# Small TensorE products held into bursts, and one transpose pass per gated block, in a two-layer hybrid encoder

## Chip, cores and metric

The kernel runs on one core of a Trainium2 chip. The metric is the device time of one execution in microseconds (us), as the median of several runs.

## What is computed

256 tokens of width 1024 pass through two layers. Each layer has a gated FFN half-step, a mixer of three branches, and a second FFN half-step; everything is float32.

```python
for i in range(DEPTH):
    h = rms_norm(x, ffn1_norm[i])
    x = x + 0.5 * (silu(h @ w_gate) * (h @ w_up)) @ w_down     # D_FF = 2816
    h = rms_norm(x, mix_norm[i])
    s5_u, gla_q, ..., at_v = split(h @ w_in[i])
    y_s5, y_gla, y_attn = s5_branch(s5_u), gla_branch(...), attn_branch(...)
    gates = sigmoid(h @ w_merge_gate[i] + b_merge_gate[i])
    x = x + sum(gate_b * (y_b @ w_branch_b)) @ w_out[i]
    x = x + 0.5 * ffn2(rms_norm(x, ffn2_norm[i]))
return rms_norm(x, final_norm)
```

The S5 branch is a bidirectional complex-diagonal state space with 32 groups of 16 channels and 64 states. Its tables (input and output matrices, powers of the decay) depend only on parameters.

## The kernel before

**Large products.** Every weight is split into two fp32r parts, `hi` (a cast on ScalarE, L209) and `lo` (a subtraction on VectorE, L210), and so is the activation. A product is three matmuls of 128x128 by 128x512 (`mm3`, L219 to L221): hi by hi, hi by lo, lo by hi. `stream` (from L223) goes through blocks of 512 output columns, loading two k-rows of weights per DMA on SP's queue (L206; five raw buffers, four cast ones), and calls the block's evacuation for each of the two token halves (t = 0, 1). In PSUM, accumulators come from a pool of three banks (`pmm`), small products from one of three (`psm`), transposes from one of two (`ptr`).

**FFN.** A block holds 256 gate and 256 up columns. Its evacuation (`evac`, L290) runs per token half: SiLU on ScalarE (L294), product on VectorE (L295), two 128x128 transposes on TensorE (L298), a cast on ScalarE (L300) and a subtraction on VectorE (L301) that write `sTh` and `sTl`, which the down product reads as activation. There are 11 blocks per FFN and four FFNs.

**S5 tables.** `s5_tables` (L529) prepares each layer's tables in four quarters of eight groups, in steps woven between the FFN's large products: layer 0's into its first FFN, layer 1's into layer 0's second FFN and layer 1's first. For a quarter VectorE makes `bb` and, from it, `tb`, which is stored in the tile that later becomes `cc`. Eight transposes (L585) go through two `psm` banks, and ScalarE copies them to `ld["bb"]` (L586). Then VectorE makes `cc`, real part first, and TensorE forms `kp`: L597 (128x32 by 128x32) and L603 (64x32 by 64x96), each as two records in the trace. ScalarE and VectorE copy `kp` to `ks` (L607 to L610), and the tables are stored to DRAM on SP's queue.

**S5 branch.** `s5` runs four quarters per layer. TensorE makes `S` (L820), VectorE multiplies, scans and multiplies again, which gives `X0` (tile `t2`) and then `X1` (`t4`). Two banks `yp` take three products for each of two halves i: `U` with `mt` (L855, 64x64), `X0` and `X1` with `cc` (L858, 128x64). `U` and `mt` are there long before, `X1` is made last. ScalarE copies `yp` to `yg` (L861), and after the fourth quarter a GELU follows.

**What sets the order.** The kernel hands its instructions to a builder that orders each engine's queue by a simulated timeline (`schedule_with_timeline_sim=True`). An instruction written earlier goes first where several are ready; one that is ready while the earlier ones are not may go ahead of them. In the mixer the branches' steps are written with raised priority (`weave` with `high_priority`); in the FFNs the tables' steps are not.

## Time and profile before

| | |
|---|---|
| median of 3 runs | 1358.05 us (1356.56 to 1358.73) |
| profiled execution | 1357.79 us |
| its span, first to last instruction | 1356.0 us |
| mean granted TensorE clock | 0.995 |
| TensorE busy | 1310.3 us, 6792 records |
| VectorE busy | 1013.2 us |
| ScalarE busy | 703.5 us |
| DMA | 249.87 MB, mean 184 GB/s |

The busy time of TensorE (PE) counts overlapping matmuls as one stretch, and the ends of matmuls are modelled. So what a matmul costs is read from the distance between starts, not from its duration. In a timeline, instructions of one form that follow one another stand as one line with their count.

### The profile page before, as it was taken

What the parts mean: (1) busy time and instruction counts of PE and PEld (TensorE: products, weight loads), DVE (VectorE), ACT (ScalarE), POOL (GpSimd) and SP (SyncE); (2) the same over time, 40 slices, a digit from 0 to 9 for tenths busy, and PEclk for the clock granted to TensorE, in tenths of its full rate; (3) what the DMA queues carried; (4) which work ended last, traced back from release to release, by engine and by line L of the source; (5) the groups of instructions that cost most, each with busy time, mean ns of one, the idle gap of its engine ahead of it and who ended that gap; (6) DMA issues with size and microseconds to landing.
All of it is one profiled execution on the core that took longest, in us unless ns stands there. A gap on an engine that the chain in (4) does not pass through costs nothing.

```text
span 1356.0 us, 19228 instructions
## 1 busy us (share of the span) xinstructions
PE 1310.3 (97%) x6792; PEld 1049.8 (77%) x6792; DVE 1013.2 (75%) x1794; ACT 703.5 (52%) x1106; POOL 76.9 (6%) x108
## 2 busy tenths in 40 slices
PE   7999999999999989999999999999999999999997
PEld 5877778877786778777877777888877867888886
DVE  6899985779995779997465765457899967655553
ACT  5545445547585445444354544355475854555542
POOL 1010220000100000210000000000001000000000
PEclk9999999999999989999999999999999999999999
DMA  7767666666452366666665655566665524555562
GB/s 230 189 214 232 219 226 189 202 223 218 163 182 78 117 161 208 196 208 215 195 196 180 196 164 189 187 177 217 226 210 156 174 68 148 191 177 181 183 209 77
DMA packets 201200, 249.87 MB, mean 184 GB/s; under 512 B 40856, under 2 KB 134600, under 8 KB 201104
## 3 DMA queue, kind: packets, MB, share of 16 engines
q1 hardware_dynamic: 200496, 247.59, 58.6%
q8 instruction: 53, 0.87, 0.3%
q10 hardware_dynamic: 608, 1.06, 0.2%
q14 instruction: 43, 0.35, 0.1%
HBM read 234.44 MB, written 13.11 MB: 183 GB/s over the span
## 4 chain that ended last, share of the span: by engine, by line
PE 58%; issue 18%; DVE 17%; DMA 4%; ACT 3%; POOL 1%; SPq 0%; POOLq 0%; ACTq 0%; DVEq 0%
PE mm L220 17%; PE mm L219 16%; PE mm L221 16%; DVE lo L210 5%; DVE t L349 2%; DMA raw<-in_ffn_w_gate 1%; DVE run L838 1%; DMA e<-scr 1%; PE as L1072 1%; PE ao L1094 1%; DVE run L837 1%; PE st L298 1%; ACT hi L209 1%; DMA raw<-in_ffn_w_up 1%; PE pt L263 1%
## 5 line engine op out<-in xcount | busy, mean ns | idle before, releaser
L210 DVE TENSOR_TENSOR lo<-raw,hi 128x1024 fp32r<-128x1024 f32 x412 | 499.0, 1218 | 178.8 <-ACT hi L209 174.1
L209 ACT CAST hi<-raw 128x1024 fp32r<-128x1024 f32 x412 | 427.8, 1043 | 309.0 <-PE mm L221 282.4
L220 PE MATMUL mm<-lo,hTh 128*128 128x512 f32 (+1 forms) x1120 | 444.0, 397 | 7.6 <-DVE lo L210 7.4
L219 PE MATMUL mm<-hi,hTh 128*128 128x512 f32 (+1 forms) x1120 | 436.4, 396 | 2.0 <-ACT hTh L267 2.0
L221 PE MATMUL mm<-hi,hTl 128*128 128x512 f32 (+1 forms) x1120 | 435.1, 392 | 0.0
L220 PEld LDWEIGHTS mm<-lo,hTh 128*128 128x128 f32 x1120 | 211.4, 189 | 53.0 <-DVE lo L210 11.9
L219 PEld LDWEIGHTS mm<-hi,hTh 128*128 128x128 f32 x1120 | 211.1, 189 | 44.4 <-ACT hTh L267 2.9
L221 PEld LDWEIGHTS mm<-hi,hTl 128*128 128x128 f32 x1120 | 210.7, 188 | 40.1 <-DVE hTl L268 0.2
L220 PE MATMUL mm<-lo,sThffn 128*128 128x512 f32 x352 | 138.3, 393 | 2.8 <-DVE lo L210 2.8
L221 PE MATMUL mm<-hi,sTlffn 128*128 128x512 f32 x352 | 137.4, 391 | 0.0
L219 PE MATMUL mm<-hi,sThffn 128*128 128x512 f32 x352 | 135.9, 393 | 0.0
L300 ACT CAST sThffn<-st 128x256 fp32r<-128x256 f32 x88 | 32.7, 372 | 129.9 <-PE st L298 129.5
L220 PEld LDWEIGHTS mm<-lo,sThffn 128*128 128x128 f32 x352 | 66.1, 188 | 17.7 <-DVE lo L210 3.7
L221 PEld LDWEIGHTS mm<-hi,sTlffn 128*128 128x128 f32 x352 | 66.1, 188 | 13.9
L219 PEld LDWEIGHTS mm<-hi,sThffn 128*128 128x128 f32 x352 | 66.0, 188 | 13.6
L301 DVE TENSOR_TENSOR sTlffn<-st,sThffn 128x256 fp32r<-128x256 f32 x88 | 37.1, 423 | 48.8 <-ACT sThffn L300 48.3
L294 ACT ACTIVATE t<-mm,rstd 128x256 f32<-128x256 f32 x88 | 41.5, 475 | 43.5 <-PE mm L221 41.1
L295 DVE SCALAR_TENSOR_TENSOR t<-mm,rstd,t 128x256 f32<-128x256 f32 x88 | 41.8, 482 | 13.6 <-ACT t L294 13.4
L298 PE MATMUL st<-ident,t 128*128 128x128 f32 x176 | 33.4, 272 | 0.5 <-DVE t L295 0.5
L298 PEld LDWEIGHTS st<-ident,t 128*128 128x128 f32 x176 | 24.3, 140 | 12.1 <-DVE t L295 0.9
L349 DVE TENSOR_TENSOR t<-e,S 128x512 f32<-128x512 f32 x32 | 20.2, 683 | 17.3 <-DMA e<-scr 17.2
L627 POOL COPY kx<-ks 128x128 f32<-128x128 f32 x32 | 18.9, 630 | 218.7 <-DVE ks L610 218.7
(357 smaller groups left out, 1440.0 us busy)
## 6 DMA issues: line engine op xcount, KB each, us to landing
raw<-in_ffn_w_gate SPq DMA_DIRECT2D x176, 256.0 KB, 3.8
raw<-in_ffn_w_up SPq DMA_DIRECT2D x176, 256.0 KB, 4.3
raw<-in_ffn_w_down SPq DMA_DIRECT2D x88, 512.0 KB, 4.6
raw<-in_w_in SPq DMA_DIRECT2D x48, 512.0 KB, 3.9
raw<-in_w_merge_gate SPq DMA_DIRECT2D x48, 512.0 KB, 4.6
raw<-in_w_out SPq DMA_DIRECT2D x16, 512.0 KB, 4.4
scr<-e SPq DMA_DIRECT2D x6, 768.0 KB, 5.5
e<-scr SPq DMA_DIRECT2D x6, 768.0 KB, 5.7
```

The source lines that it names most:

```text
L209: nc.scalar.copy(hi[:, :e - s, :width], raw[:, :e - s, :width])
L210: nc.vector.tensor_tensor(lo[:, :e - s, :width], raw[:, :e - s, :width], hi[:, :e - s, :width].bitcast(F32), op=ALU.subtract)
L219: nc.tensor.matmul(ps, act[0], w[0], start=first, stop=False)
L220: nc.tensor.matmul(ps, act[0], w[1], start=False, stop=False)
L221: nc.tensor.matmul(ps, act[1], w[0], start=False, stop=last)
L294: nc.scalar.activation(sg, ps[:, :256], AF.Silu, scale=rstd[:, t:t + 1])
L295: nc.vector.scalar_tensor_tensor(s, ps[:, 256:], rstd[:, t:t + 1], sg, op0=ALU.mult, op1=ALU.mult)
L298: nc.tensor.transpose(pt[:, j], s[:, j * P:(j + 1) * P], self.ident)
L300: nc.scalar.copy(h, pt)
L301: nc.vector.tensor_tensor(sl[:, 2 * b:2 * b + 2, t * P:(t + 1) * P], pt, h.bitcast(F32), op=ALU.subtract)
L349: self.nc.vector.tensor_tensor(out, a, b, op=ALU.mult)
L627: nc.gpsimd.tensor_copy(kx[:, :, s], ks.rearrange("p g j f -> p g (j f)")[:, :, (3 - s) * 16:(3 - s) * 16 + 64])
```

## The change

In the FFN, `evac` keeps the gated product of t = 0 until that of t = 1 is there, and then issues four transposes into one bank, those of t = 1 first, each held behind the one before; one cast and one subtraction follow. In `s5_tables`, `tb` gets a tile of its own; `kp` starts with L603 (the imaginary part, made last, first), then L597, then the eight transposes, each of the latter two held behind what was issued before; the second transposed half uses a bank of `ptr`. In `s5`, the products of `X1` come first and start the accumulation, then `X0`, then `U`. "Held" (`behind`) is an edge for the builder's order alone; it adds no wait on the chip.

```diff
+    def behind(self, m, prev):
+        self.tc.add_manual_dep(m.ins, prev.ins.name,
+                               mybir.DependencyInfo(mybir.DependencyClass.NoSync, mybir.DependencyReason.DATA),
+                               reason="one burst")
+        return m
...
             def evac(b):
+                s = []
                 def f(t, ps):
-                    self.n += 1
-                    sg, s = self.t2([P, 256]), self.t2([P, 256])
+                    sg = self.t2([P, 256])
+                    s.append(self.t2([P, 256]))
...
-                    pt = self.ptr.tile([P, 2, P], F32, name=f"st{self.n}", tag="tr")
-                    for j in range(2):
-                        nc.tensor.transpose(pt[:, j], s[:, j * P:(j + 1) * P], self.ident)
-                    h = sh[:, 2 * b:2 * b + 2, t * P:(t + 1) * P]
-                    nc.scalar.copy(h, pt)
-                    nc.vector.tensor_tensor(sl[:, 2 * b:2 * b + 2, t * P:(t + 1) * P], pt, h.bitcast(F32),
-                                            op=ALU.subtract)
+                    if t < NT - 1:
+                        return
+                    pt = self.ptr.tile([P, 2, SEQ], F32, name=self.nm("st"), tag="tr")
+                    m = None
+                    for i in range(NT - 1, -1, -1):
+                        for j in range(2):
+                            x = nc.tensor.transpose(pt[:, j, i * P:(i + 1) * P], s[i][:, j * P:(j + 1) * P], self.ident)
+                            m = self.behind(x, m) if m else x
+                    self.split_into(sh[:, 2 * b:2 * b + 2], sl[:, 2 * b:2 * b + 2], pt)
...
-            tb = ld["cc"].rearrange("p (r a e t f) -> p r a e t f", r=2, a=4, e=2, t=4)
+            tb = pp.tile([P, 2, 4, 2, 4, 16], F32, name=self.nm("tb"), tag="tb")
...
-            for i in range(2):
-                ps = self.psm.tile([P, 4, P], F32, name=self.nm("bT"), tag="sm")
-                src = tb[:, i].rearrange("p a e t f -> p a (e t f)")
-                for a in range(4):
-                    nc.tensor.transpose(ps[:, a], src[:, a], self.ident)
-                nc.scalar.copy(ld["bb"].rearrange("p (a r m) -> p r a m", a=4, r=2)[:, i], ps)
...
-            for i in range(2):
-                for a in range(4):
-                    lt = bb[:, i, 2 * a:2 * a + 2].rearrange("p e f -> p (e f)")
-                    nc.tensor.matmul(kp[0][a * 32:(a + 1) * 32, :, 0], lt, cpar[:, 2 * i, :, a], start=i == 0, stop=i == 1)
-            for i in range(2):
+            for i in (1, 0):
                 for a in range(4):
                     for d in range(2):
...
-                        nc.tensor.matmul(kp[d][a * 32:(a + 1) * 32, :, 1 - d:4 - d], lt, c5[rows, i, :, a, d:d + 3],
-                                         start=i == 0, stop=i == 1)
+                        m = nc.tensor.matmul(kp[d][a * 32:(a + 1) * 32, :, 1 - d:4 - d], lt, c5[rows, i, :, a, d:d + 3],
+                                             start=i == 1, stop=i == 0)
+            for i in range(2):
+                for a in range(4):
+                    lt = bb[:, i, 2 * a:2 * a + 2].rearrange("p e f -> p (e f)")
+                    m = self.behind(nc.tensor.matmul(kp[0][a * 32:(a + 1) * 32, :, 0], lt, cpar[:, 2 * i, :, a],
+                                                     start=i == 0, stop=i == 1), m)
+            for i in range(2):
+                pool, tag = ((self.psm, "sm"), (self.ptr, "tr"))[i]
+                ps = pool.tile([P, 4, P], F32, name=self.nm("bT"), tag=tag)
+                src = tb[:, i].rearrange("p a e t f -> p a (e t f)")
+                for a in range(4):
+                    m = self.behind(nc.tensor.transpose(ps[:, a], src[:, a], self.ident), m)
+                nc.scalar.copy(ld["bb"].rearrange("p (a r m) -> p r a m", a=4, r=2)[:, i], ps)
...
+                for r, X in ((1, X1), (0, X0)):
+                    for g, h, a, o in gh:
+                        nc.tensor.matmul(o, X[:, g * 4 + a], cc[:, r, g * 4 + a], start=r == 1, stop=False)
                 for g, h, a, o in gh:
                     rows = slice(g * 64, g * 64 + 64)
-                    nc.tensor.matmul(o, U[rows, pair[a], g], mt[rows, a], start=True, stop=False)
-                for r, X in enumerate((X0, X1)):
-                    for g, h, a, o in gh:
-                        nc.tensor.matmul(o, X[:, g * 4 + a], cc[:, r, g * 4 + a], start=False, stop=r == 1)
+                    nc.tensor.matmul(o, U[rows, pair[a], g], mt[rows, a], start=False, stop=True)
```

## Rows read from the trace of the kernel before

**Rows 1.** The page's busy times: share of the span, instructions.
```profile
PE 1310.3 (97%) x6792; PEld 1049.8 (77%) x6792; DVE 1013.2 (75%) x1794; ACT 703.5 (52%) x1106; POOL 76.9 (6%) x108
```

**Rows 2.** Timeline of TensorE around the first `kp` run: start, us, what.
```profile
112.18 0.39 PE L221 MATMUL mm<-hi,hTl 128*128 128x512 f32 x1
112.40 0.39 PE L219 MATMUL mm<-hi,hTh 128*128 128x512 f32 x1
112.72 0.56 PE L603 MATMUL kp<-cc,bb 64*32 64x96 f32 x32
...
113.55 0.40 PE L221 MATMUL mm<-hi,hTl 128*128 128x512 f32 x1
```

**Rows 3.** The same, a short run in layer 1's preparation, and the last run.
```profile
577.92 0.39 PE L219 MATMUL mm<-hi,hTh 128*128 128x512 f32 x1
578.24 0.38 PE L603 MATMUL kp<-cc,bb 64*32 64x96 f32 x10
...
578.88 0.39 PE L221 MATMUL mm<-hi,hTl 128*128 128x512 f32 x1
...
860.50 0.54 PE L603 MATMUL kp<-cc,bb 64*32 64x96 f32 x26
```

**Rows 4.** Timeline of TensorE: the `yp` products of layer 0's second quarter.
```profile
279.11 0.33 PE L855 MATMUL yp<-mt,U 64*64 64x64 f32 x2
...
279.79 0.33 PE L855 MATMUL yp<-mt,U 64*64 64x64 f32 x4
...
280.48 0.32 PE L855 MATMUL yp<-mt,U 64*64 64x64 f32 x2
...
291.40 0.45 PE L858 MATMUL yp<-cc,t 128*64 128x64 f32 x8
...
294.50 0.45 PE L858 MATMUL yp<-cc,t 128*64 128x64 f32 x8
294.88 0.34 PE L855 MATMUL yp<-mt,U 64*64 64x64 f32 x8
295.16 0.69 PE L858 MATMUL yp<-cc,t 128*64 128x64 f32 x16
295.77 0.50 PE L219 MATMUL mm<-hi,hTh 128*128 128x512 f32 x1
```

**Rows 5.** Timeline of TensorE: two and four transposes of the gated product.
```profile
44.36 0.40 PE L220 MATMUL mm<-lo,hTh 128*128 128x512 f32 x1
44.59 0.38 PE L298 MATMUL st<-ident,t 128*128 128x128 f32 x2
...
45.04 0.40 PE L219 MATMUL mm<-hi,hTh 128*128 128x512 f32 x1
...
770.94 0.39 PE L219 MATMUL mm<-hi,hTh 128*128 128x512 f32 x1
771.17 0.60 PE L298 MATMUL st<-ident,t 128*128 128x128 f32 x4
...
771.84 0.39 PE L220 MATMUL mm<-lo,hTh 128*128 128x512 f32 x1
```

**Rows 6.** Groups of VectorE by form: count, busy us, mean ns, idle before.
```profile
L301 DVE TENSOR_TENSOR sTlffn<-st,sThffn 128x256 fp32r<-128x256 f32 x88 | 37.1, 423 | 48.8 <-ACT sThffn L300 48.3
...
L681 DVE TENSOR_TENSOR mTl<-mT,mTh 128x512 fp32r<-128x512 f32 x8 | 5.3, 690 | 5.3 <-ACT mTh L680 5.3
```

**Rows 7.** Two stretches: length, busy us by engine, PEclk, DMA share, GB/s.
```profile
300.00:400.00 100.00, 96.58 (x566) 79.52 (x566) 98.25 (x156) 70.78 (x123) 6.47 (x4) 1.00 0.58 182
...
480.00:500.00 20.00, 15.73 (x68) 12.53 (x68) 15.23 (x38) 9.02 (x16) 0.69 (x1) 0.83 0.73 191
```

**Rows 8.** Waits of ScalarE: us in total, times, longest.
```profile
ACT bb L586 <- PE bT L585: 9.4, 7, 3.3
```

More of the change, by code (lines that the diff above doesn't have):

```diff
@@ L290, in evac @@
             def evac(b):
+                s = []
                 def f(t, ps):
-                    self.n += 1
-                    sg, s = self.t2([P, 256]), self.t2([P, 256])
+                    sg = self.t2([P, 256])
+                    s.append(self.t2([P, 256]))
                     nc.scalar.activation(sg, ps[:, :256], AF.Silu, scale=rstd[:, t:t + 1])
-                    nc.vector.scalar_tensor_tensor(s, ps[:, 256:], rstd[:, t:t + 1], sg, op0=ALU.mult, op1=ALU.mult)
-                    pt = self.ptr.tile([P, 2, P], F32, name=f"st{self.n}", tag="tr")
-                    for j in range(2):
-                        nc.tensor.transpose(pt[:, j], s[:, j * P:(j + 1) * P], self.ident)
-                    h = sh[:, 2 * b:2 * b + 2, t * P:(t + 1) * P]
-                    nc.scalar.copy(h, pt)
-                    nc.vector.tensor_tensor(sl[:, 2 * b:2 * b + 2, t * P:(t + 1) * P], pt, h.bitcast(F32),
-                                            op=ALU.subtract)
+                    nc.vector.scalar_tensor_tensor(s[t], ps[:, 256:], rstd[:, t:t + 1], sg, op0=ALU.mult, op1=ALU.mult)
+                    if t < NT - 1:
[7 more added lines that the diff above has]
+                    self.split_into(sh[:, 2 * b:2 * b + 2], sl[:, 2 * b:2 * b + 2], pt)
                 return f
```

## The prediction

> **What bounds the kernel now.** I read the busy times first, then TensorE's timeline around its small products, then the waits and the stretches. TensorE is busy 97% of the span, VectorE 75%, ScalarE 52% [rows 1]. A busy TensorE says nothing of its rate, so the timeline comes next. There the large products of L219 to L221 start 0.22 to 0.23 us after one another (112.18, 112.40) [rows 2]; I take 0.227. Time that is not this step is spent on small products, or waiting. So I price a run of small products as the distance from the last large one ahead of it to the second one behind it, less two steps (0.454).
>
> By that measure 32 `kp` products of L603 cost 113.55 - 112.40 - 0.454 = 0.70 us [rows 2], and ten of them cost 578.88 - 577.92 - 0.454 = 0.51 us [rows 3]. The 22 more products cost 0.19 us, 0.009 each; what is left, **0.42 us, is paid for going into these small array shapes and out again**, however few products are in the run. The same quarter's products stand in several runs: 578.24 is one of five in its quarter, while 860.50 holds 26 at once [rows 3].
>
> Transposes are different. Two cost 45.04 - 44.36 - 0.454 = 0.23 us, four cost 771.84 - 770.94 - 0.454 = 0.45 us [rows 5]: 0.11 each and no price per run. So of all that the change gathers, only the runs in a small array shape (`kp`, `yp`) are worth gathering.
>
> **The change part by part.**
>
> *Gated product (L294 to L301).* 44 blocks each had two pairs of transposes and now have one four. Per block TensorE goes from 2 x 0.23 to 0.45 us, which is 0.01 or nothing [rows 5]: 0.3 us over 44. The bounds are 0 and 0.9 (0.02 each by rounding). VectorE's 88 subtractions of 0.423 become 44 of the shape that `mTl` has now, 0.690: 37.2 - 30.4 = 6.8 us less VectorE work [rows 6]. ScalarE's casts shrink likewise. I cost both at nothing, because VectorE has slack in most of the FFNs; without that slack it would be a gain. The first token half now waits for the second. Behind it in the queues stand one cast and one subtraction, and its reader is the down product, which takes the blocks in order: even the last block is read only after 20 k-rows x 2 x 3 products x 0.227 = 27 us.
>
> *`kp` and `bT` (L580 to L604).* I count 35 runs that hold `kp` products in the timeline: 22 with L603, of which the first and the last stand in [rows 2, 3], and 13 with L597 alone. Ten lie in layer 0's preparation, 25 in layer 1's. If each of the eight quarters becomes one run, layer 0 loses six and layer 1 loses 21. Each new run has one inner change of shape (L603 to L597). Its price I take from `yp`: 16 products of L858 take 295.77 - 295.16 = 0.61 us, eight take 294.88 - 294.50 = 0.38, so 0.029 each and 0.15 for the change [rows 4]. Layer 0: 6 x 0.42 - 4 x 0.15 = **1.9 us**; layer 1: 21 x 0.42 - 4 x 0.15 = **8.2 us**. The transposes themselves cost the same wherever they stand.
>
> Whether each becomes one run is the open point. The edges that the change adds only say "not before"; nothing forbids a large product in between. In layer 0 the first L603 run is already whole (32), so there the order is nearly what is wanted. In layer 1 ten products stand alone at 578.24 although their operands were made before: they were put wherever the builder's simulated timeline had a hole. The held products can be put into holes too, one behind another. The ends are therefore 0 and 8.2; I take half, 4.1, for want of a row on either side, and half of layer 0's (1.0), since that stretch has little slack on any engine.
>
> The transposed operand gets its own tile, so `cc` can be written without waiting for transposes; that removes a possible wait and adds no instruction. The eight pairs of ScalarE copies (L586) and the stores of `bb` on SP's queue move behind the last `kp`. Weight casts (L209) stand behind the copies on ScalarE, weight loads behind the store on SP. Four cast buffers of 12 products each, 2.7 us, cover about 8 us of a late copy; five raw buffers cover more of a late store. I cost both at nothing on that cover; without it see the rival below. One `bT` bank now comes from the two that the gated product uses.
>
> *`yp` (L853 to L858).* Before, the `U` products go first, in two or three runs, half the `X0` products alone, and the rest together: 279.11, 279.79, 280.48, then 291.40, then 294.50 to 295.77 [rows 4], five runs. Over a layer I count 5 + 5 + 4 + 4 = 18. After, all of a quarter hang on the operand made last, and nothing of them can go early; they are then all ready together. 18 become 4 per layer, with one more inner change each. Quarters 0 and 1 of both layers: 16 x 0.42 - 4 x 0.15 = 6.1 us. Quarters 2 and 3: 12 x 0.42 - 4 x 0.15 = 4.4 us. In the stretch where the latter lie VectorE is busy 98.25 of 100 us [rows 7], so TensorE's time saved there may turn into waiting for VectorE: between 0 and 4.4, and I take the half, 2.2. After the last operand the run is longer (about 1.8 us instead of 1.27); the copy of L861 and the GELU behind the last quarter come up to 0.6 us later per layer, covered by branch products now, a loss of 1.2 without that cover.
>
> Here the trace and the notes part. The trace's price of an extra run is 0.42 us [rows 2, 3]. The Trainium skill, "TensorE: Matmul & The Clock Gate", section "Measured speedup vs the span model", gives packed small products the duration of one plus some 4 ns for each further one, with nothing for entering or leaving. By it a saved run is worth no more than the 0.33 us that a run of two takes (279.11), and the 13.7 us below would be about 10.8, 1347. The Trainium skill, "TensorEngine Tiling", section "Key Properties", says that a change of tiling mode drains the engine; the trace agrees with that page.
>
> **The sum.** 0.3 + 1.0 + 4.1 + 6.1 + 2.2 = 13.7 us. The profiled execution took 1357.79 us (1356.0 of span and 1.8 around it), 0.26 under the median of 1358.05. 1357.8 - 13.7 = 1344.1, and 1344.4 against the median.
>
> **The rivals.**
> 1. *All in whole bursts.* Layer 1 gives its 8.2, layer 0 its 1.9, VectorE gives way: 0.3 + 1.9 + 8.2 + 10.5 = 20.9 us, 1337. The whole runs of 32 and 26 speak for it, the five pieces of one quarter against. A wait can go with it: between 480 and 500 us TensorE is busy 15.7 of 20 us, and its granted clock is 0.83 of full (2.4 GHz) there, so partly at the lower level of 1.2 GHz [rows 7]. It comes from the order at that border, which any change can move; without it another 5 us go, 1332.
> 2. *It doesn't do what it says.* Holes still split what is held, the layer 1 preparation gains nothing, and the saturated stretch eats quarters 2 and 3: 0.3 + 1.0 + 6.1 = 7.4 us, 1350.6. If VectorE eats half of that too, no change remains to be seen.
> 3. *Slower: held copies stop ScalarE.* The `bT` copies already kept ScalarE idle seven times, 9.4 us, 3.3 at the longest [rows 8], but covered. Now the products ahead of them come later, up to 26 us in the quarter around 578. If ScalarE's order was planned on an earlier arrival, weight casts stand behind it and TensorE runs out of weights. At 3.3 us past the cover for each of the eight quarters, 26 us are lost: 1344.4 + 26.4 = 1371. It decides from 1.7 us per quarter (13.7 / 8). Against it: the builder plans with the same edges, and today's waits never reached TensorE.
>
> **How the numbers follow.** The forecast (1341 to 1349) gets 0.42 (0.08 of it for the smaller price per run, 1347), rival 1 (1330 to 1341) 0.19, rival 2 (1349 to 1355.3) 0.16, its end of no visible change 0.12, rival 3 0.11. About 0.2% (2.7 us) is what a measurement of this kernel can tell from no change, so same is 1355.3 to 1360.8. Faster 0.77, same 0.12, slower 0.11. The range 1333 to 1358 leaves out rival 3, some 0.05 of the middle, and 0.04 below.
>
> **What would show it.** Right: TensorE's timeline has four runs of `yp` per layer, of 48 records each, costing about 2.0 us; far fewer than 35 runs with `kp`; L298 in fours; 44 of L300 near 0.59 us and of L301 near 0.69. The price per run stays at 0.42. Wrong: `kp` still in five pieces per quarter in layer 1 (rival 2); VectorE full in 300 to 400 and longer waits of L220 for L210 there; ScalarE idle before L586 for tens of us with L219 waiting for L209 (rival 3). A new wait of several us at a border between stages, with a lower granted clock behind it, would make the number wrong without touching the reasons.

## The result and the profile after

| | before | after |
|---|---|---|
| median | 1357.93 us (1356.56 to 1358.73, 4 runs) | 1369.04 us (1367.74 to 1374.16, 4 runs) |
| profiled execution | 1357.79 us | 1374.16 us |
| span, mean granted clock | 1356.0 us, 0.995 | 1372.3 us, 0.986 |

The ratio is 1.0088 [1.0069, 1.0106]: the change makes the kernel 11 us slower, where 13.7 us of gain were forecast. The profiled execution is the slowest of its four, 5 us over their median, so the stretches below add up to more than 11.

First the busy times of the page of after, which answer to [rows 1].

```profile
PE 1313.6 (96%) x6792; PEld 1060.4 (77%) x6792; DVE 1009.5 (74%) x1750; ACT 694.2 (51%) x1062; POOL 96.3 (7%) x108
```

TensorE, VectorE and ScalarE hardly moved. GpSimd (POOL) did: 76.9 us became 96.3 with the same 108 instructions, and the last experiments come back to it. The timeline shows that the edits do what they say. A quarter's tables in layer 0's preparation, to be held against [rows 2]:

```profile
112.89 0.40 PE L228 MATMUL mm<-hi,hTl 128*128 128x512 f32 x1
113.22 0.56 PE L606 MATMUL kp<-cc,bb 64*32 64x96 f32 x32
...
113.97 1.09 PE L618 MATMUL bT<-ident,tb 128*128 128x128 f32 x8
...
115.14 0.40 PE L227 MATMUL mm<-lo,hTh 128*128 128x512 f32 x1
```

All 48 `kp` records and the eight transposes stand together and cost 115.14 - 112.89 - 0.454 = 1.80 us. Layer 1's preparation, against [rows 3], still has pieces of two:

```profile
774.50 0.39 PE L226 MATMUL mm<-hi,hTh 128*128 128x512 f32 x1
774.82 0.35 PE L606 MATMUL kp<-cc,bb 64*32 64x96 f32 x2
...
775.43 0.39 PE L228 MATMUL mm<-hi,hTl 128*128 128x512 f32 x1
```

Two products alone cost 775.43 - 774.50 - 0.454 = 0.48 us. In all, 35 runs that hold `kp` became 22, and 36 that hold `yp` became eight. The gated product's cast (582 ns) and subtraction have the forecast sizes (groups by form, against [rows 6]), and the copies of `bT` wait less than before, not more (waits of ScalarE, against [rows 8]):

```profile
L696 DVE TENSOR_TENSOR sTlffn<-st,sThffn 128x512 fp32r<-128x512 f32 x44 | 30.1, 685 | 17.2 <-ACT sThffn L695 17.0
```

```profile
ACT bb L619 <- PE bT L618: 6.1, 5, 2.1
```

So rival 3 is not what happened. The loss shows in the waits of TensorE (in total, times, longest):

```profile
PE mm L227 <- DVE lo L217: 14.3, 12, 3.1
...
PE glu L904 <- ACT ysh L695: 5.4, 2, 2.7
...
PE yTp L883 <- ACT yg L879: 1.8, 2, 0.9
```

The first of these was 10.2 us in eleven waits before; the last two did not exist. **Where they stand** is found by the start times of the large products (L226 to L228). There are 4896 in both traces, in the same order of work: 792 make an FFN, 624 w_in and the gates, 240 the branches and w_out. The table gives, for each stretch of them, how much longer (+) or shorter it took than in the profiled execution of before. The first column counts from the start of the span, and the first product itself starts up to 1.6 us later in one execution than in another. The rest of a mixer begins at the last gate product. The kernels below the first are those of the experiments.

| us against before | FFN ahead of mixer 1 | w_in, gates 1 | rest of mixer 1 | two FFNs between | w_in, gates 2 | rest of mixer 2 |
|---|---|---|---|---|---|---|
| after | +9.4 | -8.1 | **+12.1** | -4.5 | -4.6 | **+12.3** |
| e1, `yp` alone | +0.8 | -8.6 | +10.5 | -0.8 | -6.8 | +13.2 |
| e2, `kp` alone | -0.8 | -1.2 | 0.0 | -7.6 | +1.5 | +0.2 |
| e3, gated product alone | +5.0 | -2.2 | +1.4 | -0.4 | +1.4 | +0.2 |
| e4, without `yp` | +9.1 | -1.3 | -0.3 | -6.9 | +2.0 | +0.2 |
| e8, as e4, `e` in two buffers | +2.0 | +0.2 | -2.7 | -5.5 | +2.9 | -2.5 |
| e17, as e4, `kx` on ScalarE | +1.0 | -2.2 | -0.3 | -9.6 | +2.5 | +0.2 |
| e11, after, `e` in two buffers | +2.5 | -8.5 | +10.9 | -7.4 | -4.6 | +12.0 |
| e9, `yp` in `ptr` | +0.4 | +3.4 | +0.7 | +0.3 | +6.3 | +0.9 |
| e13, as e9, `e` in two buffers | +0.3 | -3.8 | -0.5 | +0.7 | -1.4 | -0.3 |
| e12, after with both | +3.2 | -3.5 | -0.5 | -6.6 | -1.9 | -0.2 |
| e18, as e12, `kx` on ScalarE | +1.2 | -2.6 | -0.5 | -8.9 | -0.5 | -0.2 |

The loss has two places: the first FFN, in which layer 0's tables are made (9.4 us), and the end of both mixers, right behind the gates (24 us, of which 12.7 had been won ahead of it; part of both is only work of S5 that moved behind the gates). The timeline of TensorE at the first of these ends:

```profile
400.32 1.09 PE L883 MATMUL yTp<-ident,yg 128*128 128x128 f32 x8 [0.91 <-ACT yg L879]
404.13 0.79 PE L904 MATMUL glu<-ysh,hi 128*128 128x256 f32 x2 [2.72 <-ACT ysh L695]
...
409.42 0.41 PE L906 MATMUL glu<-ysh,lo 128*128 128x256 f32 x1
409.63 0.41 PE L904 MATMUL glu<-ysh,hi 128*128 128x256 f32 x1
...
410.15 0.28 PE L904 MATMUL glu<-ysh,hi 128*128 128x256 f32 x1
410.27 0.28 PE L905 MATMUL glu<-ysl,hi 128*128 128x256 f32 x1
```

The last `yp` was issued at 397.1, and no large product is left here. It is followed by the copy, the GELU, a transpose and a cast, and TensorE waits for them; then the products of `glu` come 0.21 us apart, and 0.12 from 410. Before, all of them came 0.11 to 0.12 us apart (393.4 to 398.8). The stretch (columns as in [rows 7]):

```profile
400.00:420.00 20.00, 16.28 (x97) 14.28 (x98) 15.08 (x35) 15.29 (x35) 0.70 (x1) 0.83 0.23 70
```

Behind the idle time of 2.72 us the granted clock is at its lower level (1.2 GHz) for about 6 us, which is the factor of nearly two in the distances.

### The profile page after: what moved, and what is told of

The parts are those of the page before. It is cut to its first block, busy times and chain, and to the rows that moved or that the text cites. A ratio compares the mean times of both kernels' runs of the same rounds, so it can differ in the third digit from the quotient of the medians.

```text
span 1372.3 us, 19152 instructions
## 1 busy us (share of the span) xinstructions
PE 1313.6 (96%) x6792; PEld 1060.4 (77%) x6792; DVE 1009.5 (74%) x1750; ACT 694.2 (51%) x1062; POOL 96.3 (7%) x108
## 4 chain that ended last, share of the span: by engine, by line
PE 62%; issue 17%; DVE 13%; ACT 3%; DMA 3%; POOL 2%; SPq 1%; POOLq 0%; ACTq 0%; DVEq 0%
PE mm L227 17%; PE mm L226 17%; PE mm L228 17%; DVE lo L217 4%; DMA scr<-e 1%; PE S L835 1%; ACT hi L216 1%; PE ao L1109 1%; PE as L1087 1%; PE yp L870 1%; DMA raw<-in_ffn_w_up 1%; DVE run L853 1%; PE pt L270 1%; DVE t L304 1%; POOL e L632 1%
## 5 line engine op out<-in xcount | busy, mean ns | idle before, releaser
L226 PE MATMUL mm<-hi,hTh 128*128 128x512 f32 (+1 forms) x1120 | 433.9, 395 | 3.6 <-ACT hTh L274 2.2
L228 PE MATMUL mm<-hi,hTl 128*128 128x512 f32 (+1 forms) x1120 | 434.6, 391 | 0.0
L226 PEld LDWEIGHTS mm<-hi,hTh 128*128 128x128 f32 x1120 | 211.7, 189 | 48.9 <-ACT hTh L274 3.5
L228 PEld LDWEIGHTS mm<-hi,hTl 128*128 128x128 f32 x1120 | 211.7, 189 | 42.2 <-DVE hTl L275 0.2
L228 PE MATMUL mm<-hi,sTlffn 128*128 128x512 f32 x352 | 138.7, 394 | 0.0
L226 PE MATMUL mm<-hi,sThffn 128*128 128x512 f32 x352 | 136.7, 394 | 0.0
L228 PEld LDWEIGHTS mm<-hi,sTlffn 128*128 128x128 f32 x352 | 66.9, 190 | 14.0
L226 PEld LDWEIGHTS mm<-hi,sThffn 128*128 128x128 f32 x352 | 66.9, 190 | 13.9
L304 DVE SCALAR_TENSOR_TENSOR t<-mm,rstd,t 128x256 f32<-128x256 f32 x88 | 41.4, 479 | 11.5 <-ACT t L303 11.3
L642 POOL COPY kx<-ks 128x128 f32<-128x128 f32 x32 | 29.8, 973 | 233.7 <-DVE ks L625 157.4
L696 DVE TENSOR_TENSOR sTlffn<-st,sThffn 128x512 fp32r<-128x512 f32 x44 | 30.1, 685 | 17.2 <-ACT sThffn L695 17.0
L695 ACT CAST sThffn<-st 128x512 fp32r<-128x512 f32 x44 | 25.6, 582 | 25.4 <-PE st L312 25.3
L632 POOL TENSOR_TENSOR e<-r,tcst 128x512 f32<-128x512 f32 x8 | 18.8, 2349 | 140.7 <-DVE r L361 80.1
L270 PE MATMUL pt<-ident,x 128*128 128x128 f32 x96 | 16.7, 314 | 11.6 <-DVE t L272 8.3
```

The costliest lines, as they stand in the source:

```text
L226: nc.tensor.matmul(ps, act[0], w[0], start=first, stop=False)
L228: nc.tensor.matmul(ps, act[1], w[0], start=False, stop=last)
L270: nc.tensor.transpose(pt[:, k], self.x[:, t, (4 * c + k) * P:(4 * c + k + 1) * P], self.ident)
L304: nc.vector.scalar_tensor_tensor(s[t], ps[:, 256:], rstd[:, t:t + 1], sg, op0=ALU.mult, op1=ALU.mult)
L632: nc.gpsimd.tensor_tensor(ld["e"][:, SCR_R - SCR_E:].rearrange("p (g c) -> p g c", g=GQ), self.r4[:, gs].unsqueeze(2).to_broadcast((P, GQ, ...
L642: nc.gpsimd.tensor_copy(kx[:, :, s], ks.rearrange("p g j f -> p g (j f)")[:, :, (3 - s) * 16:(3 - s) * 16 + 64])
```

## The experiments

The theories grew with the runs. **Theory A**: the `yp` part loses because S5's chain ends after the last gate product. **The store**: the gated product loses because VectorE waits for a store in layer 0's preparation. **Theory G**, formed last: the store is late because GpSimd is held up. The other rivals are named in the expectations, whose letters are given anew from one set of runs to the next (in that of e8, Theory G is the store itself). The results, each against runs of before on the same chip (medians 1357.9 to 1359.2 us):

| | `kp` | gated product | `yp` order | `yp` banks | `e` buffers | median us | ratio to before |
|---|---|---|---|---|---|---|---|
| after | new | new | new | psm | 1 | 1369.04 | 1.0088 [1.0069, 1.0106] |
| e1 | old | old | new | psm | 1 | 1366.70 | 1.0068 [1.0054, 1.0083] |
| e2 | new | old | old | psm | 1 | 1350.10 | 0.9947 [0.9933, 0.9961] |
| e3 | old | new | old | psm | 1 | 1364.52 | 1.0053 [1.0040, 1.0066] |
| e4 | new | new | old | psm | 1 | 1363.64 | 1.0036 [1.0022, 1.0050] |
| e5 | new | old | U first | psm | 1 | 1352.91 | 0.9965 [0.9955, 0.9976] |
| e6 | new | old | new, S ahead | psm | 1 | 1366.07 | 1.0065 [1.0050, 1.0080] |
| e8 | new | new | old | psm | 2 | 1352.12 | 0.9955 [0.9940, 0.9969] |
| e9 | old | old | new | ptr | 1 | 1367.93 | 1.0072 [1.0058, 1.0086] |
| e10 | new | old | new | ptr | 1 | 1363.16 | 1.0038 [1.0024, 1.0052] |
| e11 | new | new | new | psm | 2 | 1361.55 | 1.0023 [1.0010, 1.0037] |
| e12 | new | new | new | ptr | 2 | 1347.48 | 0.9922 [0.9910, 0.9934] |
| e13 | old | old | new | ptr | 2 | 1354.27 | 0.9977 [0.9964, 0.9990] |
| e14 | new | old | new | ptr | 2 | 1348.65 | 0.9942 [0.9927, 0.9957] |
| e15 | old | old | old | psm | 2 | 1357.40 | 0.9991 [0.9980, 1.0002] |
| e16 | new | old | old | psm | 2 | 1350.08 | 0.9948 [0.9934, 0.9962] |
| e17, `kx` on ScalarE | new | new | old | psm | 1 | 1351.48 | 0.9949 [0.9934, 0.9964] |
| e18, `kx` on ScalarE | new | new | new | ptr | 2 | **1346.14** | 0.9906 [0.9892, 0.9921] |

### The parts alone: e1 to e4

Each of e1 to e3 is the kernel before with one part of the change's diff (e1 the order in `s5`, of which the diff below shows one line, e2 `kp` and `bT` in `s5_tables`, e3 `evac`). e4 is the kernel after with the old order in `s5`, this diff turned round; a further single run of it (e7) took 1361.11 us.

```diff
-                for r, X in enumerate((X0, X1)):
+                for r, X in ((1, X1), (0, X0)):
```

> The kernel before with the S5 part of the change alone (X1 first, then X0, then U). Theory A (the yp products now take their two banks of the pool of three only when X1 is there, the next quarter's S and everything behind it in that pool come later, the S5 chain ends after the last gate product and its tail stands open): slower by 9 to 13 us, 1367 to 1371; the first S product of the second quarter starts some 14 us later relative to the large products than before (20 us after, instead of before, the first quarter's X1); TensorE waits for glu as in the changed kernel, with the granted clock falling behind it. Rival B (the loss comes from the held kp products and their late copies): faster by 5 to 10 us, 1348 to 1353. Rival C (a long run of small products itself lowers the granted clock): slower, with the clock falling at the yp runs and no idle stretch ahead of the fall.

> The kernel before with the table part alone (tb of its own, L603, L597, transposes held one behind another). Theory A: faster by 2 to 5 us, 1353 to 1356, from fewer runs in both preparations; mixers as before. Rival B (held products delay ScalarE's copies and the weights behind them): slower by 5 to 12 us, with new waits of L220 for L210 in the first FFN.

> The kernel before with the gated product's part alone (four transposes in one bank, one cast, one subtraction). Theory A and the recorded sum: within 2 us of before, 1356 to 1360, since four transposes cost what two pairs do. Rival D (the later cast and subtraction, or a changed order of the weight casts around them, cost the first FFN the 5 to 10 us that it lost): slower by 4 to 10 us, most of it before 220 us.

> The changed kernel with the S5 part undone (U, X0, X1 as before), the table part and the gated product's part kept. Theory A: 9 to 13 us faster than the changed kernel, 1356 to 1360, and no wait of TensorE for glu. Rival B or D: within 3 us of the changed kernel, 1366 to 1372.

Measured: `yp` alone 8 us slower, `kp` alone 8.7 us faster by the medians (7.2 by the ratio), the gated product alone 5.8 us slower; `kp` with the gated product 4.9 us slower. By these medians **one part is good and two are bad**, and the gated product's loss seems to grow beside `kp`: -8.7 and +5.8 would make -2.9. By the ratios, -7.2 and +7.2 would make 0 against +4.9, and with the intervals that is barely clear of noise. `yp` alone and `kp` alone moved the way that Theory A forecast, the one a little less than its range, the other more than it; the gated product went as rival D had it; e4 lies between the ranges. e1 has both tail waits of after, with the clock falling behind them and not at the runs of `yp` (its rival C), so the mixers' loss is that of the `yp` part alone. e4 has none of them and keeps the first FFN's +9.1.

The place of that +9.1 shows in VectorE's and then TensorE's timeline, here of after:

```profile
167.84 0.69 DVE L381 TENSOR_TENSOR e<-U,U 128x512 f32<-128x512 f32 x1 [3.92 <-DMA scr<-e]
...
169.90 2.35 DVE L217 TENSOR_TENSOR lo<-raw,hi 128x1024 fp32r<-128x1024 f32 x2
```

```profile
171.16 0.79 PE L227 MATMUL mm<-lo,sThffn 128*128 128x512 f32 x1 [3.13 <-DVE lo L217]
171.76 0.63 PE L228 MATMUL mm<-hi,sTlffn 128*128 128x512 f32 x1
172.18 0.63 PE L226 MATMUL mm<-hi,sThffn 128*128 128x512 f32 x1
```

VectorE is to write the next quarter's `e` into the one buffer, whose last content is still on its way to DRAM. The weight subtractions stand behind it in its queue, and TensorE waits 3.1 us for one. The records behind it are 0.42 us apart (171.76 to 172.18) instead of 0.23: the lower clock again. The wait is new: in after VectorE has 8.8 us in three waits for this store, before it had none.

### The wait for the store: e8, e11

e8 is e4, and e11 is after, with a second buffer for tile `e`.

```diff
-        return {name: self.ld.tile([P, z - a], F32, name=self.nm(name), tag="s5" + name) for name, (a, z) in SCR_AT.items()}
+        return {name: self.ld.tile([P, z - a], F32, name=self.nm(name), tag="s5" + name, bufs=2 if name == "e" else 1) for name, (a, z) in SCR_AT.items()}
```

> The changed kernel with the S5 part undone and two buffers for the tile e. Theory G (in layer 0's preparation VectorE waits for the store of e before it may write the next quarter's e, weight subtractions stand behind it, and TensorE starves): the waits of VectorE for the store are gone, the 8 to 10 us lost before 220 us come back in large part, 1350 to 1356; the mixers, where e is loaded, may gain too, which the stretches show. Rival H (the first FFN loses its time to the merged transposes themselves): still 1360 to 1366, and the first 220 us as slow as in the changed kernel.

> The whole change, tile e with two buffers and nothing else. If VectorE's wait for the store of e accounts for what the gated product loses, this takes off what two buffers took off without the yp part (11.5 us of 1363.6): 1369 - 11.5 = 1357.5, and what remains against 1350.1 of kp alone is the yp part's 8 us. Rival: the order of the builder moves anyway and the wait comes back elsewhere: 1365 or more.

e8 takes 11.5 us off e4. The wait and the stretch around it in e4:

```profile
DVE e L381 <- DMA scr<-e: 5.1, 3, 4.3
```

```profile
165.00:170.00 5.00, 0.41 (x1) 0.41 (x2) 3.74 (x4) 1.91 (x3) 1.56 (x1) 0.89 0.61 235
```

and the same five microseconds of e8, in whose waits there is no line with this store:

```profile
165.00:170.00 5.00, 5.00 (x24) 4.14 (x23) 5.00 (x8) 2.64 (x4) 1.71 (x1) 1.00 1.04 397
```

The first FFN's loss falls from 9.1 to 2.0 us. e11 takes 7.5 us off after, where 11.5 were expected, and nearly all of it in the same FFN (9.4 to 2.5); both tails stay at 11 and 12 us. So the store is what most of the first loss comes through, and not the second.

### The order of yp: e5, e6, e9, e10

e5 puts `U` first and `X1`, `X0` together; e6 keeps the change's order and writes the next quarter's `S` ahead of `yp`; both with `kp` new (`first` issues a quarter's products of `S`). e9 (on before) and e10 (with `kp` new) take the change's order and the two `yp` tiles from the pool of transposes. The diffs, in part, are those of e5 (against before, where `U` is first too), of e6, and of e9 and e10.

```diff
-                for r, X in enumerate((X0, X1)):
+                for r, X in ((1, X1), (0, X0)):
                     for g, h, a, o in gh:
-                        nc.tensor.matmul(o, X[:, g * 4 + a], cc[:, r, g * 4 + a], start=False, stop=r == 1)
+                        nc.tensor.matmul(o, X[:, g * 4 + a], cc[:, r, g * 4 + a], start=False, stop=r == 0)
```

```diff
+            if q < NQ - 1:
+                nx = tiles("bb")
+                self.s5_load(l, q + 1, nx, "bb")
+                S = first(q + 1, nx["bb"])
```

```diff
-            yp = [self.psm.tile([P, 2, 4, 16], F32, name=self.nm("yp"), tag="sm") for _ in range(2)]
+            yp = [self.ptr.tile([P, 2, 4, 16], F32, name=self.nm("yp"), tag="tr") for _ in range(2)]
```

> The table part alone (1350 us in the run before this) and in the S5 part U first again, with X1 and X0 together behind it. Theory A (the S5 chain came late because the two yp banks are granted only when X1 is there, with the next quarter's S behind them): U takes the banks early as in the kernel before, S stands where it stood, no wait for glu, and eight runs of X0 alone are saved at 0.42 us: 1345 to 1349. Rival E (it is the later X0, or the longer run after X1, that makes the chain late): slower than the table part alone by 5 us or more, 1355 to 1360, with waits for glu.

> The table part, the changed S5 part (X1 first), and the next quarter's S written ahead of this quarter's yp, so that its banks stand ahead in the pool. Theory A: S of the second quarter starts before the first quarter's X1 is there, the chain is no longer late, no wait for glu: 1340 to 1347. Rival F (banks are not the matter; a product that is ready only when its turn has passed the last hole simply comes late): as the table part with the S5 part, 1358, TensorE still waits for glu.

> The yp order of the change alone, with its two banks taken from the pool of transposes (ptr) instead of from psm, so that the next quarter's S no longer stands behind them for a bank. Theory A (the loss comes from the banks: yp takes its banks late, S behind it comes late, the chain ends with nothing left to cover it): S of the second quarter starts by large product 985 instead of 1020 to 1040, the last yp comes before 1390, no wait of L889 for ysh, and the 8 to 10 us that the four whole runs per layer save are kept: 1348 to 1352. Rival B (in the mixers VectorE sets the pace, so that time saved on TensorE there turns into waits): no wait of L889 either, but TensorE waits for lo (L210) and for S grow by as much as the runs save: 1355 to 1360. Rival C (the pool of transposes becomes the new jam: the attention's and the gated linear branch's transposes stand behind yp): new waits of several us for qkT, keT or goT, 1360 or more.

> kp and yp parts of the change, yp's banks from ptr, the gated product as before. Theory A: the gains add, kp alone was 8.6 us, yp in ptr 7 to 10: 1340 to 1344. Rival B: like kp alone, 1348 to 1352. If the parts disturb one another as kp and the gated product did: 1353 or more.

The chain first, in the timeline of after, first layer:

```profile
280.35 0.45 PE L870 MATMUL yp<-cc,t 128*64 128x64 f32 x8
280.74 0.49 PE L835 MATMUL S<-U,bb 128*128 128x128 f32 x2
...
289.02 1.05 PE L835 MATMUL S<-U,bb 128*128 128x128 f32 x8
```

The second quarter's `S` comes with the first quarter's `yp`, at 280.7 and 289.0. Before, the two halves started at 260 and 275. (After runs some 9 us late here, from the first FFN; e1, which does not, has them at 272.7 and 281.0.) Every later quarter inherits that, and the last `yp` comes at 395, right after the last gate product (394.4); before it came at 380, with some 40 large products still to go. In e9 all 16 products of this `S` start at 262, the last `yp` at 383, and the waits of `glu` and `yTp` are gone: **the banks are what delayed the chain**, as Theory A has it. Rival C of e9 is out too: TensorE waits 1.1 us for `goT` there, 1.4 before, and not at all for `qkT` and `keT`. e6 shows the same from the other side (`S` at 262, no wait of `glu`).

But neither is faster. In e6 a new wait comes in place of the old: the second `yp` bank comes free only when VectorE has read the `S` ahead of it.

```profile
297.74 0.69 PE L876 MATMUL yp<-cc,t 128*64 128x64 f32 x8 [3.69 <-DVE t L356]
```

In e9 and e10 the next thing is late: the `e` of the next quarter, which the mixer loads into the same single buffer. VectorE's timeline in e9, with a weight subtraction next in its queue (275.38):

```profile
273.57 1.88 DVE L349 TENSOR_TENSOR t<-e,S 128x512 f32<-128x512 f32 x3 [3.12 <-DMA e<-scr]
```

Such waits were there before the change too, and longer in total (17.2 us in four against 9.4 in three). That they cost nothing then because the order around them was planned on a later `S` is inferred; that they cost something now, e13 will show. VectorE's waits in before:

```profile
DVE t L349 <- DMA e<-scr: 17.2, 4, 5.1
```

e5 is a miss of another kind: it splits `yp` into fewer runs without holding `U` back, has no wait of `glu`, and is 2.8 us slower than e2 (the intervals just overlap). TensorE now waits 4.2 us in three waits ahead of `S` (L830) until VectorE has read the one before. That is as much as its fewer runs save by the prediction's price (28 in place of 36, 8 x 0.42 = 3.4 us).

### Both mends: e12 to e16

e13 is e9, and e12 is after with `yp` from `ptr`, both with two buffers of `e`. e14 is e12 with the old `evac`. e15 is before, and e16 is e2, with two buffers of `e` and nothing else. The edits are those shown above.

> The whole change with both mends: two buffers of e, yp's banks from ptr. Theory A with the e wait as second cause: 1352.1 (kp, gated product, two e) less 7 to 10 for whole yp runs: 1342 to 1346, about what was forecast. Rival B: 1350 to 1354. If neither mend reaches the cause: over 1358.

> The yp order alone, its banks from ptr, and tile e with two buffers. In the run with the banks alone VectorE stood 9.4 us in three waits for the load of e, up to 3.5 each, and weight subtractions stood behind it. Theory A2 (yp's late banks and the single buffer of e are two waits in a row, and only with both gone the whole runs pay): no wait of VectorE for e, no wait of L889 for ysh, 1347 to 1352. Rival B (VectorE's work itself limits the mixer): 1355 to 1360. If the buffer has no part in it: 1366 to 1369 again.

> kp and yp parts with both mends, the gated product as before. Against the whole change with both mends (1347.5) only the gated product's part differs. Theory A2 with the gated product as a loss even with two buffers of e: 1341 to 1345. If the gated product is worth nothing once e has two buffers: 1346 to 1349. Rival (the parts again disturb one another): over 1350.

> The kernel before with two buffers of e and nothing else, as the measure for what the mend alone is worth. In before VectorE stands 17.2 us in four waits for the load of e. Theory A2: most of that is covered, 1352 to 1357, so that the gains of the mended kernels are the change's own. Rival: the buffer is the whole gain of the mended kernels, 1345 to 1350.

> The kp part with two buffers of e, yp and the gated product as before. If the buffer's worth adds to that of kp alone (1350.1): 1345 to 1348. If kp alone never met that wait: 1349 to 1351.

The whole change with both mends takes 1347.48 us, ratio 0.9922 [0.9910, 0.9934]: 10 us below the kernel before and 22 below the kernel after, and its waits of TensorE hold neither `glu` nor `yTp`. It lies between its first range and that of rival B. The second buffer is no gain by itself (e15: 0.9991 [0.9980, 1.0002]; e16 is like e2). `yp` alone needs the banks and the buffer: with the banks alone 1367.93, with both 1354.27, so its loss of 8 us turns into a gain of 4. That is less than Theory A2 asked for (1347 to 1352). Beside `kp` it is less still: e16 to e14 is 1350.08 to 1348.65, with intervals that overlap. Yet a whole run costs what was forecast, here the third quarter in e13:

```profile
311.04 0.39 PE L220 MATMUL mm<-lo,hTh 128*128 128x512 f32 x1
311.36 0.69 PE L855 MATMUL yp<-cc,t 128*64 128x64 f32 x16
...
313.47 0.40 PE L219 MATMUL mm<-hi,hTh 128*128 128x512 f32 x1
```

313.47 - 311.04 - 0.454 = 1.98 us. Part of the rest goes as rival B of e13 has it: in the same mixer VectorE does four scans in a row ahead of a weight subtraction, and TensorE waits and then runs at the lower clock.

```profile
345.57 1.21 DVE L837 TENSOR_TENSOR_SCAN run<-e,t 64x511 f32<-64x511 f32 x1
...
351.48 1.22 DVE L210 TENSOR_TENSOR lo<-raw,hi 128x1024 fp32r<-128x1024 f32 x1
```

```profile
352.75 0.60 PE L220 MATMUL mm<-lo,hTh 128*128 128x512 f32 x1 [2.65 <-DVE lo L210]
353.15 0.63 PE L221 MATMUL mm<-hi,hTl 128*128 128x512 f32 x1
```

The gated product, which cost 5.8 us alone and 13.5 beside `kp` (e4 against e2), shows nothing clear once `e` has two buffers: with `yp` mended it is 1.2 us faster (e14 to e12: 1348.65 to 1347.48), with the old `yp` 2 us slower (e16 to e8: 1350.08 to 1352.12), both with intervals that overlap.

### Why the store is late: e17, e18

Before, a store of `e` was issued at 151.84 us, and VectorE's next write of `e` came at 162.76. The store had landed by 158.05, when GpSimd, which waits for it too, began its part:

```profile
151.84 0.34 SPq L624 DMA_DIRECT2D scr<-e  x1
```

In after it is issued at 160.59, although VectorE's part of its data was made at 155. SP's queue in after:

```profile
154.68 1.62 SPq L645 DMA_DIRECT2D scr<-kx  x3
...
160.59 0.41 SPq L639 DMA_DIRECT2D scr<-e  x1
```

The stores of `kx`, from 154.68 to 159.5, stand ahead of it and wait for GpSimd, which copies `ks` to `kx` (L642) and makes the last part of `e` (L632). GpSimd's timeline in after, and the durations of these 32 copies (shortest, median, longest ns) in after and in before:

```profile
145.06 9.59 POOL L642 COPY kx<-ks 128x128 f32<-128x128 f32 x4 [18.64 <-DVE ks L625]
154.62 1.48 POOL L632 TENSOR_TENSOR e<-r,tcst 128x512 f32<-128x512 f32 x1
```

```profile
L642 POOL COPY kx<-ks x32: 287/298/8391, 118.4 to 872.4; 128x128 f32<-128x128 f32 x32
```

```profile
L627 POOL COPY kx<-ks x32: 286/747/1704, 115.6 to 863.8; 128x128 f32<-128x128 f32 x32
```

The longest of them, 8.39 us for a copy that takes 0.29 elsewhere, begins at 145.06 and ends at 153.45. VectorE meanwhile does twelve operations without a break, each with both operands in SBUF, and the copy ends under the first that has one operand in PSUM, the subtraction of `sTlffn`:

```profile
144.93 0.67 DVE L376 TENSOR_TENSOR U<-ef,eg 128x512 f32<-128x512 f32 x1
...
153.23 0.68 DVE L696 TENSOR_TENSOR sTlffn<-st,sThffn 128x512 fp32r<-128x512 f32 x1
```

Before, the longest took 1.70 us from 141.4 and ended at 143.1, again under such a subtraction (142.89 to 143.31); its four copies at that place:

```profile
141.43 3.33 POOL L627 COPY kx<-ks 128x128 f32<-128x128 f32 x4 [23.46 <-DVE ks L610]
```

The Trainium skill, "SBUF — State Buffer", section "Who interferes with whom", says that a VectorE instruction with two SBUF inputs and a GpSimd instruction that reads SBUF shut one another out for the whole of an instruction. The trace agrees, and shows that the exclusion can outlast one instruction: here it went on through all twelve. It need not. From 184.44 on in the same trace four copies, right behind another instruction of GpSimd, took 0.75, 1.29, 0.75 and 0.75 us, each while VectorE went from one operation of that kind to the next. In e4 a copy of 5.49 us (from 579.7) ended under an operation with both operands in SBUF. What decides between the two is not shown. The merged gated product has 44 subtractions from PSUM in place of 88 [rows 6], so fewer openings for GpSimd (the 88 products of L304, which read PSUM too, stay). In every trace with the merged product and these copies on GpSimd (after, e3, e4, e7, e8, e11, e12) the copy at this place takes 8.38 or 8.39 us, in every one with the old `evac` 1.49 to 1.71. A long copy need not cost anything: with two buffers of `e` there is one of 9.25 us even without any part of the change (e15, from 177). e17 is e4 with one line changed, and e18 is e12 with the same:

```diff
-                nc.gpsimd.tensor_copy(kx[:, :, s], ks.rearrange("p g j f -> p g (j f)")[:, :, (3 - s) * 16:(3 - s) * 16 + 64])
+                nc.scalar.copy(kx[:, :, s], ks.rearrange("p g j f -> p g (j f)")[:, :, (3 - s) * 16:(3 - s) * 16 + 64])
```

> kp and the gated product as in e4, one buffer of e, and the 32 copies of kx on ScalarE instead of GpSimd. Theory G (the first cause behind the late store is GpSimd: one copy of kx takes 8.4 us because VectorE does one operation with two SBUF operands after the other, and it ends each time under the subtraction of sTlffn, whose one operand is in PSUM; the merged gated product has half as many of these, so the copies end late, and the stores of kx, the weight loads and the store of e stand behind them on SP's queue): the store of e leaves some 5 us earlier, VectorE's wait for it goes below 1.5 us in all, the first FFN loses 0 to 2 us instead of 9.1, the median is 1350 to 1355. Rival (the store is late by SP's own order, or VectorE just comes sooner; only a second buffer helps): the wait stays at 4 to 5 us, 1361 to 1365.

> The whole change with both mends, as e12, and the copies of kx on ScalarE. Theory G: what is left of the gated product's loss in the first FFN (3.2 us in e12, where one copy of kx still takes 11.5 us) goes: 1344 to 1346.5. If these copies are covered once e has two buffers: 1346.5 to 1348.5. If ScalarE's queue suffers: over 1349.

e17 takes 12 us off e4 with one buffer of `e`, and is level with `kp` alone (0.9949 against 0.9947). The first FFN's loss goes from 9.1 to 1.0 us, the store of `e` is issued at 152.42 (158.86 in e4), and VectorE's wait for it, 5.1 us in e4, is now:

```profile
DVE e L381 <- DMA scr<-e: 0.8, 1, 0.8
```

So the store is late because of the copies on GpSimd, and the rival that only a second buffer helps is out. That the missing subtractions are what holds these copies up is read from the traces and was not tested by itself. Nor was `kx` moved with the gated product alone (e3): there VectorE waits only 2.3 us for the store, so how much of its 5.8 us goes through this chain stays open. e18 has the lowest median, 1346.14 us. It lies just inside its first expectation, but its interval overlaps that of e12, and the FFNs between gave more of the difference than the first one.

## Why the prediction was wrong

It said 1344.4 us, at 0.77 faster; 1369.04 was measured, outside the range. Step by step:

- **The measure and the price per run were right.** The price of a `yp` run (2.0 forecast, 1.98 measured), two `kp` products alone (0.48), four transposes in a run (0.45, from 43.90 to 44.80 in after): all close to what was worked out. The choice between the trace's price and that of the Trainium skill, "TensorE: Matmul & The Clock Gate", section "Measured speedup vs the span model", had no part in the error.
- **`kp` and `bT`: right in sign, undersized in layer 1.** Forecast 1.0 + 4.1 of at most 10.1; alone it gave 8.7 us by the medians (7.2 by the ratio). By stretches it was 0.8 in layer 0 and 7.6 in the FFNs of layer 1's tables. Layer 1's quarters were still split, as rival 2 has it, but 25 runs became 15 there in e2. By the price that is 10 x 0.42 - 4 x 0.15 = 3.6 us; TensorE's waits for `lo` in these FFNs fell from 2.8 to 0.3 us besides, and the rest stays open.
- **`yp`: the step that failed first.** The prediction held: "After, all of a quarter hang on the operand made last, and nothing of them can go early; they are then all ready together", and looked behind them only at the copy and the GELU, "a loss of 1.2 without that cover". It missed what else moves with the first product: the two banks. The next quarter's `S` stands behind them in a pool of three, so the whole chain moved, not its end alone. In place of a gain of 8.3 us (6.1 + 2.2) the part lost 8 alone; with both waits mended it gains 4 alone and 1.4 beside `kp`. The cover that it named, products behind the chain, is just what ran out: the last `yp` met the last gate product.
- **A second wait lay behind the first.** With the banks mended, VectorE's wait for `e` held the loss (e9 to e13: 1367.93 to 1354.27), and such waits were in the trace of before, 17.2 us of them. The prediction read TensorE's timeline and never listed VectorE's waits in that stretch.
- **The gated product: "I cost both at nothing" failed, not by the slack that it named.** The sum counted VectorE's work and not which operands it has. With the 44 subtractions that fell away went openings in which GpSimd got its copies done (so the traces read); the copies, the stores behind them on SP's queue, the write of `e` and the weight subtractions came late one after the other. The part cost 13.5 us beside `kp`, where moving the copies took the loss away, and 5.8 alone, where that was not tried. The prediction looked at SP's queue only for the stores of `bb`, and at GpSimd not at all. With the copies off GpSimd the part costs what was forecast, nothing that shows (e17).
- **The rivals.** Rival 3 named the wrong engine (its copies waited 6.1 us instead of 9.4) but the right kind: a queue in order, stopped by a late input, with weight work behind it. That its 1371 us lies near the measured time is luck. The last sentence of the prediction ("a new wait of several us at a border between stages, with a lower granted clock behind it") describes the tail; it got no chance of its own, and it was to leave the reasons untouched, while here the wait came out of one of them, the `yp` part.
- With these waits taken away the change gives 10.5 us (e12), and 13 with `kx` on ScalarE (e18; what that move alone gives to before was not run). This is near the forecast's 13.7 by luck: most of it is `kp` (7 to 9 us where 5.1 were forecast), and `yp` gives 1 to 4 where 8.3 were.

What stays open: how the remaining waits for `lo` in the mixers could go (the scans' place in VectorE's queue was not tried), why the gated product costs more beside `kp` (13.5 us against 5.8 by the medians, 12 against 7 by the ratios), and where all of its loss alone comes from.

## What to carry to other kernels

When a product is made to wait for its last operand, follow what its first instruction takes besides TensorE's time: the bank it is granted then, and who is next for a bank of that pool. When VectorE's work is merged, ask which of its instructions left GpSimd an opening, and what stands behind GpSimd on the queues. A list of the waits of every engine in the stretch, also of covered ones, tells which comes up next.

## What the runs showed of the hardware

One copy of GpSimd that is held up for 8.4 us (in e12 even 11.5) by VectorE's work, as above, was not expected. Nor was this: a wait of TensorE for about 2 us does not always bring the clock down. Before, it waited 2.04 us at 149 us, and the next records kept their step; in e9, whose order on TensorE is the same up to there, it waited 2.00 us at the same place, and the records behind it are 0.43 us apart. Before, then e9:

```profile
149.15 0.50 PE L220 MATMUL mm<-lo,sThffn 128*128 128x512 f32 x1 [2.04 <-DVE lo L210]
149.49 0.40 PE L221 MATMUL mm<-hi,sTlffn 128*128 128x512 f32 x1
149.72 0.40 PE L219 MATMUL mm<-hi,sThffn 128*128 128x512 f32 x1
```

```profile
149.04 0.55 PE L220 MATMUL mm<-lo,sThffn 128*128 128x512 f32 x1 [2.00 <-DVE lo L210]
149.38 0.63 PE L221 MATMUL mm<-hi,sTlffn 128*128 128x512 f32 x1
149.81 0.63 PE L219 MATMUL mm<-hi,sThffn 128*128 128x512 f32 x1
```

Between the start and the end of the kernel the lower level came, in the traces of this case, behind one idle stretch of 1.8 us or more, and never behind a run of small products. There is one exception: in e3 it came at 406.0, behind idle stretches of only 1.10 and 0.35 us, which before has as well, at 401.0 and 401.8, and without a fall. So a new wait costs its own length and, sometimes, an estimated 1.7 to 3.4 us more: half of the time at the lower level, which is 3.4 us in e13 (352.7 to 356.1) and 6.8 in after (0.83 over 20 us).
